# A split-precision transformer trunk: making the low part of each weight tile with ScalarE and an accumulating DMA in place of a VectorE subtraction

## The chip, the cores and the metric

The kernel runs on one core of one Trainium2 chip. The metric is the device time of one execution in microseconds (us). The program is given to five engines: PE (TensorE, matmuls), DVE (VectorE), ACT (ScalarE), POOL (GpSimd) and SP (SyncE, which here only issues DMAs).

## The reference, cut to what matters

Two layers of a causal decoder with 512 tokens of 1024 features, float32 in and out.

```python
for l in range(2):
    h = rmsnorm(x, norm_mix_g[l])
    x = x + (pool_conv_mixer(h, ...) if l % 2 == 0 else mla_attention(h, cos, sin, ...))
    x = x + memory_cross_attention(rmsnorm(x, norm_xa_g[l]), rmsnorm(mem, norm_mem_g[l]), ...)
    x = x + conv_ffn(rmsnorm(x, norm_ffn_g[l]), w_up, conv_w, conv_b, w_down)   # 1024 -> 2 * 2816 -> 1024
return rmsnorm(x, final_norm_g)
```

All linear maps are dense float32 products. The mixer holds a pooling branch and a convolution of width 31 over 512 channels; the attention of layer 1 has 16 heads; the cross-attention of both layers reads 256 memory tokens through 4 heads of 256 features.

## The kernel before

Activations lie with features on the 128 partitions and tokens along the free axis, as tiles of 128 x 512. A product runs on PE in the fast `float32r` form, which rounds its operands; to keep the precision each operand is split into a high part (the value rounded to `float32r`) and a low part (the value minus the high part). `mm3` adds three matmuls for each 128 x 128 block of weights: high by high (L157), high by low of the activations (L158), and the weights' low part by the activations' high part (L159). The low part of the weights is thus wanted as the third matmul of a tile.

Weights come in tiles of up to 128 x 1024 float32 (512 KB, eight blocks, 24 matmuls of 512 columns). `load_raw` loads one from HBM into `wr` on SP's queue (4 buffers). `load_w` makes `wh` with ACT's copy (L152) and `wl` with DVE's subtraction (L153), 3 buffers each. A buffer of `wh` comes free after the last L158 matmul of the tile three before, a buffer of `wl` after its last L159 matmul. Both lines stand under a raised priority (`AHEAD` = 40 places), so that the scheduler puts them ahead of the neighbouring work on their engines; each engine then runs its own list in order. `Linear` calls `load_w` for each tile (`lin`, and `kx` for the memory keys of layer 1); `memory_kv` calls it for the memory values (`vx`); `group` calls it for the attention's query and key weights (`uqp`, `ukv`, `uqn`). The keys of layer 0 (`kx` at L340) use the raw tile alone, and the last product (`fin`) makes its own parts at L529 and L530.

In time the kernel has these stages: the opening product and the rest of the mixer's input product, the memory keys and values of both layers beside the convolution on DVE, the mixer's output product, cross-attention, the gated MLP of layer 0 (`ffn_up`, `ffn_down`), the latent attention of layer 1, its cross-attention, the MLP of layer 1 with the final norm.

Of the kernel before, what the change touches and what calls it, by code (L numbers as in the profile page):

```python
# [15 lines left out]
ALU = mybir.AluOpType  # L16
# [47 lines left out]

# columns of the packed per-channel constants
_COLS = {}
# [15 lines left out]
def _split_2pi():  # L82
    """2*pi*512 and 2*pi cut into parts whose products with the counts below are exact in float32."""
    def head(v, bits):
        m, e = math.frexp(v)
        return math.ldexp(math.floor(m * 2 ** bits), e - bits)

    big = 2.0 * math.pi * 512.0
    parts = []
    rest = big  # L90
    for _ in range(3):
        h = head(rest, 11)
        parts.append(h)
        rest -= h
    parts.append(rest)
    d1 = head(2.0 * math.pi, 13)
    return parts, (d1, 2.0 * math.pi - d1)
# [3 lines left out]
def kernel(ctx: ExitStack, tc: tile.TileContext, a):  # L101
# [26 lines left out]

# [1 line left out]
    con = cp.tile([P, NCOL], F32, tag="con", name="con")  # L130
# [9 lines left out]

# [1 line left out]
    def load_raw(src, n):  # L142
# [4 lines left out]
    def load_w(src, n):  # L147
        raw = load_raw(src, n)
        hi = wp.tile([P, WCOLS], F32R, tag="wh", name=uid("wh"), bufs=3)
        lo = wp.tile([P, WCOLS], F32R, tag="wl", name=uid("wl"), bufs=3)  # L150
        with tc.high_priority(offset=AHEAD):
            act.copy(hi[:, :n], raw[:, :n])  # L152
            vec.tensor_tensor(lo[:, :n], raw[:, :n], f(hi[:, :n]), ALU.subtract)  # L153
        return hi, lo
# [6 lines left out]
    class Linear:  # L161
        """psum[m, t] = sum over k tiles of src[p, k * 128 + m] * xs[k][p, t], a range of k at a time."""

# [36 lines left out]
    def newton_rsqrt(v, n, name):  # L200
        """1/sqrt(v) of a narrow tile."""
        sh = small(name + "sh", [P, n], dt=I32)
        y = small(name + "y", [P, n], bufs=3)
        nv = small(name + "nv", [P, n])
        t = small(name + "t", [P, n])
        vec.tensor_scalar(sh, v.bitcast(I32), 1, None, ALU.logical_shift_right)
        vec.tensor_scalar(y.bitcast(I32), sh, -1.0, float(0x5F3759DF), ALU.mult, ALU.add)
        vec.tensor_scalar(nv, v, -0.5, None, ALU.mult)
        for _ in range(3):
            vec.tensor_tensor(t, y, y, ALU.mult)  # L210
            vec.tensor_tensor(t, t, nv, ALU.mult)
            vec.scalar_tensor_tensor(y, t, 1.5, y, ALU.add, ALU.mult)
        return y

    def col_sums(acc, n=TB):
        """sums over the partitions of acc, tokens on partitions: [128, n]."""
        ps = bank("st")
        for j in range(n):
            pe.transpose(ps[:, j * P:(j + 1) * P], acc[:, j * P:(j + 1) * P], ident)
        t = small("ssum", [P, n])  # L220
        vec.reduce_sum(t, ps[:, :n * P].rearrange("p (j c) -> p j c", c=P), axis=AX.X)
        return t

    def row_rate(src, n, name):
        """1/rms of tokens whose features lie along the free axis: [128, n]"""
        parts = small(name + "p", [P, n, 2])
        for j in range(n):
            for i in range(2):
                t = slot("nat")
                sp.dma_start(t, src[j][:, i * T:(i + 1) * T])  # L230
                act.activation(t, t, AF.Square, accum_out=parts[:, j, i:i + 1])
        v = small(name + "q", [P, n])
        vec.tensor_tensor(v, parts[:, :, 0], parts[:, :, 1], ALU.add)
        vec.tensor_scalar(v, v, 1.0 / D, EPS, ALU.mult, ALU.add)
        return newton_rsqrt(v, n, name)
# [6 lines left out]
    def spread(r, n=TB, name="rb", out=None):  # L242
        """[128, n] with tokens on partitions -> [128, n * 128] with tokens along the free axis."""
        ps = bank("rb")
# [6 lines left out]
    class Norm:  # L251
        """h = x * gain as hi and lo parts and the running sum of squares, tile by tile."""

# [37 lines left out]

# [1 line left out]
    mem_rb = cp.tile([P, MEM], F32, tag="memrb", name="memrb")  # L293
# [9 lines left out]
    class Memory:  # L303
        """the memory tokens, normalised, in two stages"""

# [25 lines left out]
    def memory_kv(layer, mg, mh, keep, native, kt, vt):  # L331
        """keys [d, mem] per head and values [mem, d]; keep takes each out of PSUM; a step per weight tile"""
        for hd in range(HX):
# [40 lines left out]

# [1 line left out]
    def cross_attention(layer, norm, kv, nxt):  # L376
# [87 lines left out]

# [1 line left out]
    def ffn(layer, norm, nxt, extra=None):  # L466
# [50 lines left out]
    def finale(layer, k0, nk):  # L517
        """the last products, half of the tokens at a time, and the final norm of each half"""
        half = T // 2
# [35 lines left out]
        def upright(k):  # L555
            """x * gain of the second half with its tokens on the partitions"""
            if not nat:
# [54 lines left out]

# [1 line left out]
    def mixer(norm, nxt):  # L614
# [6 lines left out]
        def opening(i):  # L621
            """the first product starts on the first tiles of x"""
            ps = bank("lin")
# [37 lines left out]
        def convolve():  # L661
            """the causal depthwise convolution, a tap of a tile at a time"""
            todo = [list(range(CONV_K)) for _ in range(CT - 1)] + [[s for s in range(CONV_K) if s not in PE_TAPS]]
# [17 lines left out]
        def tap_products():  # L681
            """some taps of the last tile as products with a diagonal matrix"""
            ps = bank("tap")
# [11 lines left out]
        def normalise():  # L695
            """layer norm over the channels and swish, in stages"""
            acc = slot("lacc")
# [138 lines left out]

# [1 line left out]
    def rope_tables():  # L838
# [37 lines left out]

# [1 line left out]
    SWAP = [(i + 16) % 32 for i in range(32)]  # L878
    # kinds of head: rows of the content part, rows of the rotary part, rows that stay zero
    KIND = {  # L880
# [8 lines left out]
    def latent_attention(norm, nxt, cs, sn, kv):  # L889
# [4 lines left out]

        # token factors: r * rsqrt(r^2 * mean(p^2) + eps)
        def factor(sq, dim, name):
# [13 lines left out]

        # latent projections
        kacc, acc = slot("kacc"), slot("qacc")
# [37 lines left out]
        def rotate(src, buf):  # L950
            """src holds the rotary part of four heads (PSUM or SBUF); rotated into their buffers"""
            sw = slot("sw")
# [13 lines left out]
        def contents(buf, wh, wl, xs, nk):  # L966
            """content rows of two heads per 128 output rows"""
            for i, (k0, k1) in enumerate(TILE):
# [12 lines left out]
        def group(g):  # L981
            """queries and keys of four heads"""
            rotate(linear(a["uqp"][g], cq), qb)
# [48 lines left out]
        def turn(n):  # L1032
            banks = [bank("t") for _ in range(3)]
            ts = [slot("pt") for _ in range(3)]
            # key block -> bank, first column, first query block
            place = ((0, 0, 0), (1, 0, 1), (2, 0, 2), (1, 384, 3))
# [9 lines left out]
        def values(p):  # L1046
            """a pair of heads side by side in the columns of the array"""
            ps = bank("mpv")
# [31 lines left out]

# [1 line left out]
    n0 = Norm("norm_mix_g", 0)  # L1082
# [13 lines left out]

# [1 line left out]
def _chunks(w):  # L1098
    """[K, M] -> [M/128, 128 (k within its tile), K/128 * 128]"""
    k, m = w.shape  # L1100
    return w.reshape(k // P, P, m // P, P).transpose(2, 1, 0, 3).reshape(m // P, P, k)


def _cols(v):
    """[..., n * 128] -> [128, ... * n]"""
    v = np.asarray(v)
    return v.reshape(-1, P).T
# [21 lines left out]
def _layouts(inp):  # L1129
# [21 lines left out]
    out["dq"] = _chunks(np.concatenate([dq[:, :QL + KVL]] + [dq[:, QL + KVL:]] * 4, axis=1))  # L1151
    # heads of a group of four are used in the order A, C, B, D
    uq = inp["mla_w_uq"][0].reshape(KQ, P, HEADS // 4, 4, NOPE + ROPE)
# [38 lines left out]
```

## Time and profile before

| | |
|---|---|
| three runs | 1388.11, 1388.82, 1388.9 us, median 1388.82 |
| profiled execution | span 1386.6 us from the first to the last instruction; the median of the runs is 2.2 us above this span |
| PE | 1371.6 us busy (99%) |
| DVE | 889.0 us (64%), of which 276.9 are the 240 subtractions of L153 |
| ACT | 599.2 us (43%), of which 239.0 are the 240 copies of L152 |
| POOL | 6.3 us (0%) |
| DMA | 135.28 MB, mean 98 GB/s; the load queue takes 31.0% of 16 DMA engines |

Busy times count from an instruction's start to its end. Matmuls overlap, so each lasts longer than the distance to the next; the distance is read from the number of matmuls in a stretch. Idle time is put down to the engine whose signal came last. A wait of an engine that is not the bound costs nothing by itself.

### The profile page before, as it was taken

What the parts mean: (1) busy time and instruction counts of PE and PEld (TensorE: products, weight loads), DVE (VectorE), ACT (ScalarE), POOL (GpSimd) and SP (SyncE); (2) the same over time, 40 slices, a digit from 0 to 9 for tenths busy, and PEclk for the clock granted to TensorE, in tenths of its full rate; (3) what the DMA queues carried; (4) which work ended last, traced back from release to release, by engine and by line L of the source; (5) the groups of instructions that cost most, each with busy time, mean ns of one, the idle gap of its engine ahead of it and who ended that gap; (6) DMA issues with size and microseconds to landing.
All of it is one profiled execution on the core that took longest, in us unless ns stands there. A gap on an engine that the chain in (4) does not pass through costs nothing.

```text
span 1386.6 us, 16884 instructions
## 1 busy us (share of the span) xinstructions
PE 1371.6 (99%) x6532; PEld 1131.2 (82%) x6532; DVE 889.0 (64%) x1535; ACT 599.2 (43%) x976; POOL 6.3 (0%) x17
## 2 busy tenths in 40 slices
PE   8999999999999999999999999999999999999997
PEld 6888978888888888888887776888888888888887
DVE  6999988555685366445669775755566544653565
ACT  6416456443443143223447786644443322332343
POOL 0000000000000000000100000000000000000000
PEclk9999999999999999999999999999999999999999
DMA  9235524113333333333321111321223333233221
GB/s 331 93 106 188 169 91 145 61 56 98 108 97 91 105 93 93 104 91 87 97 83 50 43 46 46 107 76 61 76 91 96 102 92 106 91 93 106 84 84 62
DMA packets 42560, 135.28 MB, mean 98 GB/s; under 512 B 4848, under 2 KB 6512, under 8 KB 42480
## 3 DMA queue, kind: packets, MB, share of 16 engines
q1 hardware_dynamic: 41904, 133.45, 31.0%
q8 instruction: 51, 0.84, 0.2%
q10 hardware_dynamic: 576, 0.76, 0.2%
q14 instruction: 29, 0.24, 0.1%
HBM read 132.09 MB, written 2.10 MB: 97 GB/s over the span
## 4 chain that ended last, share of the span: by engine, by line
PE 90%; DVE 7%; ACT 2%; issue 1%; DMA 0%; SPq 0%; DVEq 0%; ACTq 0%
PE lin L159 24%; PE lin L157 24%; PE lin L158 24%; DVE cv L677 3%; PE s L1016 1%; PE mpv L1053 1%; DVE wl L153 1%; PE t L1041 1%; PE vx L158 1%; PE vx L159 1%; PE fin L157 1%; PE vx L157 1%; PE fin L158 1%; PE fin L159 1%; ACT p L1024 1%
## 5 line engine op out<-in xcount | busy, mean ns | idle before, releaser
L152 ACT CAST wh<-wr 128x1024 fp32r<-128x1024 f32 (+3 forms) x240 | 239.0, 998 | 485.0 <-PE lin L158 338.4
L157 PE MATMUL lin<-hh,wh 128*128 128x512 f32 x976 | 382.4, 392 | 5.9 <-ACT hh L264 5.9
L158 PE MATMUL lin<-hl,wh 128*128 128x512 f32 x976 | 381.1, 391 | 0.0
L159 PE MATMUL lin<-hh,wl 128*128 128x512 f32 x976 | 380.8, 390 | 0.2 <-DVE wl L153 0.2
L153 DVE TENSOR_TENSOR wl<-wr,wh 128x1024 fp32r<-128x1024 f32 (+3 forms) x240 | 276.9, 1155 | 60.4 <-ACT wh L152 58.9
L157 PEld LDWEIGHTS lin<-hh,wh 128*128 128x128 f32 x976 | 183.8, 188 | 43.2 <-ACT hh L264 5.9
L158 PEld LDWEIGHTS lin<-hl,wh 128*128 128x128 f32 x976 | 183.7, 188 | 39.4 <-DVE hl L265 2.1
L159 PEld LDWEIGHTS lin<-hh,wl 128*128 128x128 f32 x976 | 183.7, 188 | 38.7 <-DVE wl L153 0.7
L158 PE MATMUL lin<-fl,wh 128*128 128x512 f32 x304 | 118.4, 389 | 0.0
L159 PE MATMUL lin<-fh,wl 128*128 128x512 f32 x304 | 118.3, 389 | 0.0
L157 PE MATMUL lin<-fh,wh 128*128 128x512 f32 x304 | 118.1, 389 | 0.0
L514 DVE TENSOR_TENSOR x<-x,lin 128x512 f32<-128x512 f32 x32 | 22.0, 688 | 102.8 <-PE lin L159 102.8
L479 DVE TENSOR_TENSOR g<-lin,rb 128x512 f32<-128x512 f32 x44 | 30.4, 690 | 79.2 <-PE lin L159 79.2
L677 DVE SCALAR_TENSOR_TENSOR cv<-a,con,cv 128x509 f32<-128x509 f32 (+25 forms) x115 | 79.5, 728 | 0.1
L490 DVE TENSOR_TENSOR g<-lin,rb 128x512 f32<-128x512 f32 x44 | 30.4, 691 | 71.6 <-PE lin L159 71.4
L158 PEld LDWEIGHTS lin<-fl,wh 128*128 128x128 f32 x304 | 57.1, 188 | 12.1 <-DVE fl L197 0.2
L157 PEld LDWEIGHTS lin<-fh,wh 128*128 128x128 f32 x304 | 57.1, 188 | 11.8
L159 PEld LDWEIGHTS lin<-fh,wl 128*128 128x128 f32 x304 | 57.1, 188 | 11.7
L488 ACT ACTIVATE c<-c 128x512 f32<-128x512 f32 x44 | 27.8, 633 | 82.1 <-DVE c L487 82.1
L289 DVE TENSOR_TENSOR x<-x,lin 128x512 f32<-128x512 f32 x40 | 27.3, 686 | 35.6 <-PE lin L159 35.6
L158 PE MATMUL lin<-ol,wh 128*128 128x512 f32 x128 | 50.1, 391 | 0.0
L159 PE MATMUL lin<-oh,wl 128*128 128x512 f32 x128 | 49.9, 390 | 0.0
(351 smaller groups left out, 2062.4 us busy)
## 6 DMA issues: line engine op xcount, KB each, us to landing
wr<-in_ffn_up SPq DMA_DIRECT2D x88, 512.0 KB, 3.5
wr<-in_ffn_down SPq DMA_DIRECT2D x32, 512.0 KB, 3.5
wr<-in_xa_wk SPq DMA_DIRECT2D x16, 512.0 KB, 3.7
wr<-in_xa_wv SPq DMA_DIRECT2D x16, 512.0 KB, 4.2
wr<-in_xa_wq SPq DMA_DIRECT2D x16, 512.0 KB, 3.6
wr<-in_xa_wo SPq DMA_DIRECT2D x16, 512.0 KB, 3.5
wr<-in_ffn_down SPq DMA_DIRECT2D x16, 384.0 KB, 3.1
wr<-in_pc_in SPq DMA_DIRECT2D x11, 512.0 KB, 6.6
```

Source lines behind the costliest of these rows:

```text
L152: act.copy(hi[:, :n], raw[:, :n])
L153: vec.tensor_tensor(lo[:, :n], raw[:, :n], f(hi[:, :n]), ALU.subtract)
L157: pe.matmul(ps, ah, bh, start=first, stop=False)
L158: pe.matmul(ps, ah, bl, start=False, stop=False)
L159: pe.matmul(ps, al, bh, start=False, stop=last)
L289: vec.tensor_tensor(x[m], x[m], ps, ALU.add)
L479: vec.tensor_tensor(g, gps, rb, ALU.mult)
L488: act.activation(c, c, AF.Silu)
L490: vec.tensor_tensor(g, aps, rb, ALU.mult)
L514: vec.tensor_tensor(x[m], x[m], ps, ALU.add)
L677: vec.scalar_tensor_tensor(cv[i][:, s:], gl[i][:, :T - s], w, cv[i][:, s:], ALU.mult, ALU.add)
L1016: pe.matmul(ps[i], q[:, i * P:(i + 1) * P], k[:, :P * (i + 1)], start=True, stop=True)
```

## The change

In `load_w` ACT writes minus the weights into `wl`, which rounds to minus the high part, and a DMA on POOL's queue then adds the raw weights to it, read once more from HBM. DVE no longer touches the weights (comments that were taken out are left away):

```diff
         with tc.high_priority(offset=AHEAD):
             act.copy(hi[:, :n], raw[:, :n])
-            vec.tensor_tensor(lo[:, :n], raw[:, :n], f(hi[:, :n]), ALU.subtract)
+            act.mul(lo[:, :n], raw[:, :n], -1.0)
+            pool.dma_start(lo[:, :n], src, accum_op=ALU.add)
         return hi, lo
```

The new lines shift all later line numbers by one. `act.mul` is an ACTIVATE at L153, the accumulating DMA stands at L154. There are 240 tiles: 205 of 1024 columns, 12 of 768, 19 of 512, 4 of 384, 118.0 MB in all.

In the gated MLP, ACT's list held one copy for each weight tile (`wh`), between the convolution's affine step (`c`, L485), its SiLU (L488) and the split of the product (`fh`, L196):

```order
L152 CAST wh_4403<-wr_4401 128x1024
L196 CAST fh_4321<-c_4283 128x512
L152 CAST wh_4441<-wr_4439 128x1024
L485 ACTIVATE c_4358<-g_4356,con 128x512
L488 ACTIVATE c_4358<-c_4358 128x512
L152 CAST wh_4478<-wr_4476 128x1024
```

The same place now (an earlier pass of the same loop):

```order
L152 CAST wh_4278<-wr_4276 128x1024
L153 ACTIVATE wl_4279<-wr_4276 128x1024
L197 CAST fh_4194<-c_4155 128x512
L152 CAST wh_4317<-wr_4315 128x1024
L153 ACTIVATE wl_4318<-wr_4315 128x1024
L486 ACTIVATE c_4232<-g_4230,con 128x512
L489 ACTIVATE c_4232<-c_4232 128x512
L152 CAST wh_4355<-wr_4353 128x1024
L153 ACTIVATE wl_4356<-wr_4353 128x1024
```

The negation stands right behind the copy of the same tile, and the MLP's own steps come one instruction later.

POOL's list held the identity, a constant for the mixer's norm (`om`), the causal mask and the zeros of the attention's buffers, with nothing between them:

```order
masks.py:199 AFFINE_SELECT ident<-ident 128x128
L702 MEMSET om_1609 128x128
L891 MEMSET mask_5519 128x512
L892 AFFINE_SELECT mask_5519<-mask_5519 128x128
L948 MEMSET qA_5847 32x512
```

Now the DMAs stand among them, here at the start:

```order
masks.py:199 AFFINE_SELECT ident<-ident 128x128
L154 DMA wl_94<-in_pc_in 128x512
L154 DMA wl_133<-in_pc_in 128x512
L154 DMA wl_174<-in_pc_in 128x1024
L154 DMA wl_206<-in_pc_in 128x1024
L154 DMA wl_298<-in_pc_in 128x1024
```

POOL issues 240 DMAs that were not there; each waits for ACT's negation of its tile.

SP's list of loads in the opening was, with `x` the input by features, `wr` weights of the mixer's input product, and `nat` the input by tokens, from which the first norm's rate is made:

```order
L628 DMA x_78<-in_xT 128x512
L144 DMA wr_169<-in_pc_in 128x1024
L144 DMA wr_200<-in_pc_in 128x1024
L144 DMA wr_291<-in_pc_in 128x1024
L230 DMA nat_207<-in_xN 128x512
L230 DMA nat_210<-in_xN 128x512
```

and is now:

```order
L629 DMA x_78<-in_xT 128x512
L144 DMA wr_171<-in_pc_in 128x1024
L144 DMA wr_203<-in_pc_in 128x1024
L144 DMA wr_295<-in_pc_in 128x1024
L144 DMA wr_373<-in_pc_in 128x1024
L144 DMA wr_411<-in_pc_in 128x1024
L144 DMA wr_449<-in_pc_in 128x1024
L231 DMA nat_211<-in_xN 128x512
```

Three weight loads have moved ahead of the eight `nat` loads.

ACT's list at the same place was as follows (`hh` is the high part of a tile of `x` times the gain, `dg` a diagonal for the convolution):

```order
L264 ACTIVATE hh_152<-x_77,con 128x512
L687 ACTIVATE dg_770<-ident,con 128x128
L264 ACTIVATE hh_160<-x_78,con 128x512
L152 CAST wh_171<-wr_169 128x1024
L152 CAST wh_202<-wr_200 128x1024
```

and is now:

```order
L265 ACTIVATE hh_154<-x_77,con 128x512
L152 CAST wh_173<-wr_171 128x1024
L153 ACTIVATE wl_174<-wr_171 128x1024
L152 CAST wh_205<-wr_203 128x1024
L153 ACTIVATE wl_206<-wr_203 128x1024
L265 ACTIVATE hh_162<-x_78,con 128x512
```

The last tile of `x` (`hh_162`) stands behind the fourth weight tile (`wh_205`, `wl_206`), whose buffers are those of the first tile. PE's own list is the same products in nearly the same order.

## The prediction

> **What bounds the kernel now.** I read the page's first two parts, then the stretches, then the chain and the waits. The page says first which engine has no time to give:
>
> ```profile
> span 1386.6 us, 16884 instructions
> PE 1371.6 (99%) x6532; PEld 1131.2 (82%) x6532; DVE 889.0 (64%) x1535; ACT 599.2 (43%) x976; POOL 6.3 (0%) x17
> DMA  9235524113333333333321111321223333233221
> GB/s 331 93 106 188 169 91 145 61 56 98 108 97 91 105 93 93 104 91 87 97 83 50 43 46 46 107 76 61 76 91 96 102 92 106 91 93 106 84 84 62
> ...
> q1 hardware_dynamic: 41904, 133.45, 31.0%
> ...
> PE 90%; DVE 7%; ACT 2%; issue 1%; DMA 0%; SPq 0%; DVEq 0%; ACTq 0%
> ```
>
> PE stands still for 1386.6 - 1371.6 = 15.0 us in all. The chain of work that ended last is PE for 90% and DVE for 7%. The DMA engines are busy for a third, except in the first slice and around the fourth and fifth. A busy PE need not be a full one, so I take the stretches, with the count of matmuls behind PE's busy time:
>
> ```profile
> 0.00:35.00 35.00, 28.84 (x114) 22.01 (x115) 21.66 (x38) 23.05 (x43) 0.71 (x6) 1.00 0.93 331
> 107.00:177.00 70.00, 69.94 (x398) 61.27 (x397) 69.60 (x92) 37.79 (x53) 0.00 (x0) 1.00 0.55 178
> 310.00:680.00 370.00, 370.00 (x1637) 306.29 (x1637) 210.22 (x278) 128.68 (x158) 2.08 (x4) 1.00 0.32 96
> 735.00:840.00 105.00, 104.28 (x561) 76.55 (x560) 84.64 (x263) 83.77 (x193) 0.00 (x0) 1.00 0.18 55
> ```
>
> The columns after the length are PE, PEld, DVE, ACT, POOL, the clock, the DMA share and GB/s. In the gated MLP (310 to 680) a matmul comes every 370 / 1637 = 0.226 us without a gap. A weight tile of 24 matmuls lasts 24 x 0.226 = 5.42 us there, and DVE has 43% to spare. So taking work off DVE buys nothing in the MLPs; what matters is whether `wl` still arrives in time. In the opening the DMA engines are the full resource: 331 GB/s at a share of 0.93, or 331 / 0.93 = 356 GB/s if they never rest. By this a full tile of 0.524 MB takes 0.524 / 356 = 1.47 us of all 16 engines.
>
> **The change, part by part.** What moves, and what prices it:
>
> ```profile
> L152 ACT CAST wh<-wr 128x1024 fp32r<-128x1024 f32 (+3 forms) x240 | 239.0, 998 | 485.0 <-PE lin L158 338.4
> L153 DVE TENSOR_TENSOR wl<-wr,wh 128x1024 fp32r<-128x1024 f32 (+3 forms) x240 | 276.9, 1155 | 60.4 <-ACT wh L152 58.9
> ...
> wr<-in_ffn_up SPq DMA_DIRECT2D x88, 512.0 KB, 3.5
> ...
> nat<-in_xN SPq DMA_DIRECT2D x8, 256.0 KB, 7.2
> ...
> wr<-in_pc_in SPq DMA_DIRECT2D x2, 256.0 KB, 4.1
> ```
>
> 1. DVE loses 240 instructions, 276.9 us. ACT gains 240 of the same shapes as its copies, 239.0 us, to 838 of 1387 (60%). ACT waits 338.4 us for PE in front of the copies, and PE's bound hides the rest outside the attention.
>
> 2. POOL gains 240 DMAs of 118.0 MB. No POOL-issued and no adding DMA is in this trace. I call r the engine time of one against a plain load of the same bytes. It is not below 1, since it carries the same bytes in. At the far end reading the weights, reading what stands in `wl`, adding and writing cost a whole plain transfer each, r = 4. I take r = 2, because such a DMA has two inbound streams where the rows show one. Landing is then the plain 3.5 us, plus 1.47 for the second stream, plus up to 1.47 when a raw load shares the engines: 6.4 us. For POOL's issue I take 1.0 us, between SP's 0.33 and the 1.9 at which SP's full queue issues (9.35 us for 5 in the opening):
>
> ```profile
> 15.56 9.35 SPq L144 DMA_DIRECT2D wr<-in_pc_in  x5
> 507.25 1.05 ACT L152 CAST wh<-wr 128x1024 fp32r<-128x1024 f32 x1 [3.06 <-PE lin L158]
> 508.21 0.81 ACT L485 ACTIVATE c<-g,con 128x512 f32<-128x512 f32 x1
> 772.51 65.27 SPq L144 DMA_DIRECT2D wr<-in_mla_o  x7
> ```
>
> The Trainium skill, "DMA: Bandwidth & Descriptors" (Anatomy of one DMA), fits a POOL-issued DMA as 2.0 us plus bytes at 436 GB/s, an estimate of 3.2 us for 512 KB, which would be the hidden case below. "Collectives: The Full Stack" (The bandwidth ceiling) says a reducing DMA runs at half the rate because it needs two source reads, with a measured ratio of 1.93. It would give my sum, and nothing in this trace decides between the two pages.
>
> 3. *The MLPs and the other products with tiles of 24 matmuls.* PE releases a buffer and ACT, idle 3.06 us before, copies at once. Then 1.05 copy, 1.05 negation, 1.0 issue, 6.4 landing: 9.5 us. The low part is wanted two tiles and two matmuls later, 2 x 5.42 + 0.45 = 11.3 us. Engine time is (1 + 2) x 1.47 = 4.4 us in 5.42. So nothing is lost, with 1.8 us to spare. What stands behind the negation on ACT (`c`) goes 1.05 us later; its product is used only when its group of tiles is complete.
>
> 4. *The memory keys and values, 107 to 177.*
>
> ```profile
> 107.00:177.00 70.00, 29.20 (x25) 1.00 0.55 178
> L340 PE MATMUL kx<-mg,wr x128: 377/379/379, 75.7 to 107.2; 128*128 128x256 f32 x128
> ```
>
> The first row counts the subtractions: 25 tiles in 70 us, 2.8 us each, because a value tile feeds only 12 wide matmuls. Raw loads need 178 x 70 / 356 = 35 us of engine time, the 25 tiles 25 x 1.47 x 2 = 73.6 more: 109 in 70. Ahead of it the keys of layer 0 use raw tiles only (second row), so three tiles can be ready, 3 x 3 x 1.47 = 13 us. Lost: 109 - 70 - 13 = 26 us. Here PE waits for `wl`, and DVE, full now with 69.6 of 70, no longer matters.
>
> 5. *The mixer's output product* has 16 half tiles of 12 matmuls, 2.7 us each; the way from release to landing (0.6 + 0.6 + 1.0 + 2.0 + 3 x 0.74) is 6.4 against 2 x 2.7 + 0.45 = 5.9, a third of 0.5 for each, some 2 us.
>
> 6. *The opening.*
>
> ```profile
> 3.85 0.62 ACT L152 CAST wh<-wr 128x512 fp32r<-128x512 f32 x1 [0.90 <-DMA wr<-in_pc_in]
> 4.50 0.69 DVE L153 TENSOR_TENSOR wl<-wr,wh 128x512 fp32r<-128x512 f32 x1 [4.50 <-ACT wh L152]
> 7.32 0.63 PE L159 MATMUL lin<-hh,wl 128*128 128x512 f32 x1
> 8.29 6.87 SPq L230 DMA_DIRECT2D nat<-in_xN  x8
> 21.02 0.16 DVE L233 TENSOR_TENSOR rxq<-rxp 128x4 f32<-128x4 f32 x1 [3.38 <-ACT nat L231]
> 26.18 0.44 PE rb L246 x4
> ```
>
> The first L159 matmul starts at 7.32. Now: copy ends 4.5, negation 5.1, issue 6.1, landing 4.1 plus 0.74 later, 10.9: PE is 3.6 us late. Nine more matmuls end the first tile near 14; the fourth tile's negation waits for that and ends near 15, and the last tile of `x` stands behind it. SP's eighth weight load needs the buffer which that negation frees, and the eight `nat` loads, issued from 8.29 before, stand behind that load: 6.7 us later. The rate was ready shortly before PE used it (`rb`, 26.18). It moves by these 6.7, by some 3 for the two full accumulations that share the engines and by 2 to 3 negations among ACT's squares, less about 1.3 of slack: 11 us in all. The loads in their sum say the same: 7 full tiles x 2 x 1.47 = 20.6 us more in a stretch with 35 x 0.07 = 2.5 to spare and 9.8 of loads ahead of need.
>
> 7. *The attention, 735 to 840.* ACT gets what DVE loses here, 13 tiles and some 12 us (first row below), and goes from 83.8 to about 96 of 105 us. ACT's exponentials feed DVE and PE in turn there, so I charge half, 6.
>
> ```profile
> 735.00:840.00 105.00, 12.72 (x13) 1.00 0.18 55
> 736.58 0.95 DVE L153 TENSOR_TENSOR wl<-wr,wh 128x768 fp32r<-128x768 f32 x1
> L157 PE MATMUL nope<-cqh,wh x24: 389/389/389, 737.6 to 825.1; 128*128 128x512 f32 x24
> 747.07 1.14 DVE wl L153
> 768.84 1.13 DVE wl L153
> 771.62 0.87 DVE wl L153
> ```
>
> The first group's query tile is used 0.1 us after its subtraction (second and third row), and would land some 4 us later. Three subtractions of 3.1 us stand in the chain and go. 6 + 4 - 3 = 7 us.
>
> 8. POOL's own list: its memsets wait for DVE, and DMAs stand behind them.
>
> ```profile
> 666.08 0.52 POOL L948 MEMSET qA<- 32x512 f32 x1 [461.57 <-DVE g L490]
> 693.34 0.52 POOL L948 MEMSET kD<- 32x512 f32 x1 [4.03 <-DVE acc L275]
> ```
>
> The zeros were all written by 693.9, over 30 us before the attention's tiles are used. Cost nothing; if they came 30 us later the key tiles would hang on them.
>
> Sum: 11 + 26 + 2 + 7 = +46 us on the span of 1386.6, that is 1433. The median of the runs, 1388.82, is 2.2 above the span: 1435.
>
> **The rivals.** *The addition is dearer and the DMA engines become the bound.* It decides from r = 5.42 / 1.47 - 1 = 2.7, where a full tile no longer fits beside PE's time. At r = 3 each of some 175 full tiles outside opening and memory stage loses 0.47 (82 us), the memory stage 62, the opening 14, the rest 13: 1560. At r = 4 they are 341, 99, 17 and 25: 1871. For it: no row prices the addition. Against: one third of the engines' time is all that plain loads take.
>
> *The transfer is hidden anyway*, r near 1. The memory stage then needs 35 + 37 = 72 us, less its lead: nothing. The opening keeps 8, since the late `nat` loads hardly depend on r, the attention 5: 1402, at best 1390.
>
> *Faster.* DVE's freed time shortens the attention, the one place where its subtractions stand between PE's pieces: 3 us there, and 2 in other gaps of the 15.0 that PE has: 1384. It decides only if the opening loses under 5 us; the order of the loads speaks against that.
>
> *POOL issues late.* If an issue took 3.5 us in place of 1.0, because POOL has to wait for DVE's instructions of 0.7 to 1.2 us, the way would be 12.0, over 11.3: 0.7 / 3 for each of 175 tiles, 41 us: 1476. Against it: POOL idles now and DVE is at 64%, at 44% after. The Trainium skill, "SBUF — State Buffer" (SBUF: two separate sides), describes such a lockout of POOL's descriptor writing while DVE runs certain copies; no run here shows it yet.
>
> **How the numbers follow.** The forecast (r from 1.5 to 2.6) 49%, the dearer addition 25%, hidden 14%, faster 6%, late issue 6%. The predicted time is the likeliest case's, 1435; its own range is 1412 (r = 1.5: 10 + 7 + 0 + 6) to 1461 (r = 2.6: 13 + 48 + 3 + 8). The range of 80% goes from 1392, below which lie the faster case and a little of the hidden one, to 1750, above which lies the part of the dearer case with r over 3.6, about 10%. A measurement can tell about 0.2% from no change. Faster 0.06; same 0.05, from the hidden case; slower 0.89.
>
> **What would show it.** Right: L153 gone from DVE, an ACT group of about 240 us at `wl`, a POOL queue of about 118 MB; PE idle before L159 in the memory stage, waiting for a DMA to `wl`; `rb` near 37 us; MLP stretches still at 0.226 us a matmul. DMA share there near 0.32 x 3 = 0.96 by the rows' unhurried share, or 0.8 by 4.4 of 5.42. Wrong: PE waiting for `wl` in every MLP tile (r over 2.7, or landing over 8 us), or no wait at all in the memory stage.

## The result and the profile after

The changed kernel takes 1499.75 us, the median of four runs (1498.9 to 1502.47), against 1388.64 for the kernel before on the same chip: 1.0805 times as long (95% interval 1.079 to 1.082), 111 us slower. The forecast was 46 us slower. The direction held; the size was more than twice what I had summed. The time lies inside the wide range of 1392 to 1750 only by luck: it is above the likeliest case's own range (1412 to 1461), and the wide range reached that far for the sake of the dearer addition, which is not what happened.

The page of the changed kernel, its busy times, the granted clock, the two large DMA queues and the chain of work that ended last:

```profile
span 1497.1 us, 17423 instructions
PE 1402.3 (94%) x6532; PEld 1146.6 (77%) x6532; DVE 639.3 (43%) x1295; ACT 807.9 (54%) x1216; POOL 213.2 (14%) x257
PEclk9999799999999999999999999999999999999999
...
q0 software_dynamic: 34560, 117.98, 44.0%
q1 hardware_dynamic: 41904, 133.45, 31.0%
...
PE 50%; issue 29%; DMA 10%; POOL 4%; DVE 3%; ACT 2%; SPq 0%; POOLq 0%; DVEq 0%; ACTq 0%
```

PE now stands still for 1497.1 - 1402.3 = 94.8 us, against 15.0. It also counts 30.7 us more busy for the same 6532 matmuls, so some of them ran slower. The adding DMAs are a queue of their own (q0): 117.98 MB, or 225 full tiles, for 44.0% of the span. That is 658.7 us of all 16 engines and 2.93 us for a full tile.

The groups of the new work, and the medians from issue to landing:

```profile
L153 ACT ACTIVATE wl<-wr 128x1024 fp32r<-128x1024 f32 (+3 forms) x240 | 240.1, 1000 | 23.6 <-PE vx L159 23.6
...
L154 POOL DMA_DIRECT2D wl<-in_ffn_up x88 | 76.1, 865 | 408.2 <-ACT wl L153 401.7
```

```profile
wl<-in_ffn_up POOLq DMA_DIRECT2D x88, 512.0 KB, 7.6
...
wl<-in_xa_wv POOLq DMA_DIRECT2D x16, 512.0 KB, 7.6
...
wl<-in_xa_wk POOLq DMA_DIRECT2D x8, 512.0 KB, 8.7
...
wl<-in_pc_out POOLq DMA_DIRECT2D x16, 256.0 KB, 4.9
...
nat<-in_xN SPq DMA_DIRECT2D x8, 256.0 KB, 11.6
```

What PE waited for, in total, times, and the longest:

```profile
PE vx L159 <- DMA wl<-in_xa_wv: 22.4, 13, 7.1
PE kx L160 <- DMA wl<-in_xa_wk: 12.7, 4, 4.7
PE lin L160 <- DMA wl<-in_pc_in: 7.8, 2, 4.8
PE lin L158 <- ACT hh L265: 6.2, 1, 6.2
PE rb L247 <- DVE rmy L213: 5.3, 1, 5.3
PE lin L160 <- DMA wl<-in_mla_o: 4.7, 2, 4.4
PE nope L160 <- DMA wl<-in_uqn: 4.6, 1, 4.6
PE lin L160 <- DMA wl<-in_xa_wo: 4.3, 2, 2.2
PE lin L160 <- DMA wl<-in_pc_out: 3.8, 5, 1.3
PE rb L247 <- DVE rxy L213: 3.6, 1, 3.6
PE lin L160 <- DMA wl<-in_xa_wq: 3.5, 1, 3.5
PE lin L160 <- DMA wl<-in_ffn_up: 3.0, 1, 3.0
```

Only the wait for `hh` was there before (5.9 us). The rest are waits for a low part, or for one of the two rates of the opening (`rxy`, the first norm; `rmy`, the memory tokens). The 88 tiles of `ffn_up` cost one wait of 3.0 us in all.

To see where the time went I took the start of the same PE work in both traces. The difference of neighbouring rows is what the stage between them lost:

| event on PE | before | after | later by | lost since the row above |
|---|---|---|---|---|
| `rb` of the first norm | 26.0 | 39.5 | 13.5 | 13.5 |
| first native key product (`kx`, L341) | 75.7 | 97.1 | 21.4 | 7.9 |
| last `vx` product | 177.0 | 247.7 | 70.7 | 49.3 |
| first token sums for cross-attention (`st`) | 228.6 | 310.0 | 81.4 | 10.7 |
| first `rb` of the first MLP | 349.1 | 432.5 | 83.4 | 2.0 |
| first `nope` product of the attention | 734.9 | 824.6 | 89.7 | 6.3 |
| last `nope` product | 825.5 | 924.0 | 98.5 | 8.8 |
| last scores of the second cross-attention (`sx`) | 966.5 | 1074.1 | 107.6 | 9.1 |
| `rb` of the second MLP | 1026.0 | 1136.0 | 110.0 | 2.4 |
| last `fin` product | 1376.8 | 1486.8 | 110.0 | 0 |

Two of the rows from which the table is made, with first and last start (the native keys and the last value products):

```profile
L341 PE MATMUL kx<-mg,wr x128: 377/379/379, 97.1 to 128.6; 128*128 128x256 f32 x128
```

```profile
L160 PE MATMUL vx<-wh,ml x64: 387/393/632, 132.6 to 247.7; 128*128 128x512 f32 x64
```

Some stretches by engine, in the order of the prediction's (length, PE, PEld, DVE, ACT, POOL, clock, DMA share, GB/s), opening, memory stage, attention and second MLP:

```profile
0.00:39.50 39.50, 21.91 (x72) 16.23 (x72) 8.09 (x22) 24.84 (x43) 6.03 (x12) 0.96 0.90 274
...
128.60:247.70 119.10, 83.93 (x397) 68.48 (x396) 33.42 (x52) 59.11 (x76) 21.78 (x26) 0.89 0.90 212
...
824.60:924.00 99.40, 92.72 (x470) 68.13 (x468) 67.06 (x223) 78.06 (x176) 8.90 (x11) 0.97 0.40 89
...
1136.00:1450.00 314.00, 314.00 (x1388) 260.11 (x1387) 104.66 (x149) 155.67 (x183) 48.30 (x56) 1.00 0.89 190
```

The second MLP is as full as before: 1388 matmuls in 314 us, 0.226 us each. The memory stage is the other extreme: the 70 us have become 119.1, of which PE is idle for 35.2, and its clock is 0.89.

The chain in the memory stage shows both (start, length, what):

```profile
157.61 7.99 DMA wl<-in_xa_wv
165.60 0.04 issue
165.64 0.80 PE vx L159
166.44 0.43 PE vx L160
166.86 0.43 PE vx L159
...
169.85 0.43 PE vx L160
...
171.05 0.23 PE vx L159
...
172.89 0.24 PE vx L159
173.13 0.01 POOLq L154
173.14 7.35 DMA wl<-in_xa_wk
180.49 0.04 issue
180.54 0.39 PE kx L160
```

An addition lands at 165.6 and PE starts after 7.07 us of idleness. For 4.6 us its matmuls come 0.43 us apart in place of 0.23. The addition that goes out at 173.14 is that of the next key tile, and the chain puts its wait down to the L159 product that ends just before it. ACT's list shows what it more likely waited for, its own negation, which ends at 172.85:

```profile
170.31 1.05 ACT L152 CAST wh<-wr 128x1024 fp32r<-128x1024 f32 x1 [5.57 <-PE vx L160]
...
171.79 1.06 ACT L153 ACTIVATE wl<-wr 128x1024 fp32r<-128x1024 f32 x1
```

The three additions before it also went out 0.29 to 0.30 us after the end of their negations. PE's last product with the value tile at 165.6 releases ACT at 170.3; copy, a cast, negation, issue and landing follow, 10.2 us until 180.5. In between PE works on the tiles that are there, and then stands idle for 4.2 us.

### The profile page after: what moved, and what is told of

It reads as the page before. It is cut to its first block, busy times and chain, and to the rows that moved or that the text cites. A ratio compares the mean times of both kernels' runs of the same rounds, so it can differ in the third digit from the quotient of the medians.

```text
span 1497.1 us, 17423 instructions
## 1 busy us (share of the span) xinstructions
PE 1402.3 (94%) x6532; PEld 1146.6 (77%) x6532; DVE 639.3 (43%) x1295; ACT 807.9 (54%) x1216; POOL 213.2 (14%) x257
## 3 DMA queue, kind: packets, MB, share of 16 engines
q0 software_dynamic: 34560, 117.98, 44.0%
## 4 chain that ended last, share of the span: by engine, by line
PE 50%; issue 29%; DMA 10%; POOL 4%; DVE 3%; ACT 2%; SPq 0%; POOLq 0%; DVEq 0%; ACTq 0%
PE lin L160 13%; PE lin L158 13%; PE lin L159 13%; POOL wl L154 4%; DMA wl<-in_xa_wv 3%; DVE cv L678 2%; DMA wl<-in_xa_wk 1%; PE s L1017 1%; DMA wl<-in_xa_wo 1%; DMA nat<-in_memN 1%; PE fin L158 1%; PE fin L159 1%; PE fin L160 1%; DMA nat<-in_xN 1%; PE mpv L1054 1%
## 5 line engine op out<-in xcount | busy, mean ns | idle before, releaser
L159 PE MATMUL lin<-hl,wh 128*128 128x512 f32 x976 | 383.5, 393 | 0.0
L153 ACT ACTIVATE wl<-wr 128x1024 fp32r<-128x1024 f32 (+3 forms) x240 | 240.1, 1000 | 23.6 <-PE vx L159 23.6
L159 PEld LDWEIGHTS lin<-hl,wh 128*128 128x128 f32 x976 | 185.5, 190 | 39.0 <-DVE hl L266 0.8
L154 POOL DMA_DIRECT2D wl<-in_ffn_up x88 | 76.1, 865 | 408.2 <-ACT wl L153 401.7
L159 PE MATMUL lin<-fl,wh 128*128 128x512 f32 x304 | 118.3, 389 | 0.0
L515 DVE TENSOR_TENSOR x<-x,lin 128x512 f32<-128x512 f32 x32 | 22.0, 688 | 142.8 <-PE lin L160 142.8
L480 DVE TENSOR_TENSOR g<-lin,rb 128x512 f32<-128x512 f32 x44 | 30.4, 691 | 105.8 <-PE lin L160 98.2
L159 PEld LDWEIGHTS lin<-fl,wh 128*128 128x128 f32 x304 | 57.1, 188 | 11.9
L487 DVE SCALAR_TENSOR_TENSOR c<-g,con,c 128x511 f32<-128x511 f32 x44 | 33.1, 751 | 72.3 <-ACT c L486 72.3
L266 DVE SCALAR_TENSOR_TENSOR hl<-x,con,hh 128x512 fp32r<-128x512 f32 x48 | 36.0, 751 | 59.6 <-ACT hh L265 59.4
L154 POOL DMA_DIRECT2D wl<-in_ffn_down x40 | 34.5, 863 | 176.3 <-ACT wl L153 169.7
```

The source lines that it names most:

```text
L153: act.mul(lo[:, :n], raw[:, :n], -1.0)
L154: pool.dma_start(lo[:, :n], src, accum_op=ALU.add)
L159: pe.matmul(ps, ah, bl, start=False, stop=False)
L266: vec.scalar_tensor_tensor(l, x[k], g, f(h), ALU.mult, ALU.subtract)
L480: vec.tensor_tensor(g, gps, rb, ALU.mult)
L487: vec.scalar_tensor_tensor(c[:, 1:], g[:, :T - 1], w(1), c[:, 1:], ALU.mult, ALU.add)
```

## The experiments

The code below is shortened, and some names are changed. I had three theories. A: PE waits for a low part that lands late. B: the traffic itself makes all loads late. C: ACT's second pass is what costs. Within A, two things could set the pace: the engines' sum of time, or the way from a buffer's release to the landing, against a ring of three.

**A spare tile that nobody reads.** DVE subtracts for PE as before; ACT and the DMA do the new work beside it.

```diff
+            vec.tensor_tensor(lo[:, :n], raw[:, :n], f(hi[:, :n]), ALU.subtract)
-            act.mul(lo[:, :n], raw[:, :n], -1.0)
-            pool.dma_start(lo[:, :n], src, accum_op=ALU.add)
+            act.mul(spare[:, :n], raw[:, :n], -1.0)          # 3 buffers, SLOTS = 53
+            pool.dma_start(spare[:, :n], src, accum_op=ALU.add)
```

> DVE makes the low parts that PE uses, as before; ACT's negation and the adding DMA work as in the changed kernel, but on a spare tile (3 buffers; the working slots are 53 in place of 58 to make room) that nobody reads. So the traffic, ACT's load and POOL's queue stay and only PE's wait for the DMA goes. Theory A (PE's wait for the late low part costs nearly all): 1395 to 1420 us, with some 10 to 20 us left in the opening, where the loads stand in another order. Theory B (the traffic itself costs, because raw loads come late): over 1470. Theory C (ACT's second pass costs): over 1440.

Measured: 1493.06 us, 1.0757 (1.0737 to 1.0776). Theory A's range is missed, and those of B and C are met: though PE reads nothing that an addition writes, the kernel is almost as slow. ACT's group and its largest waits in this run:

```profile
L155 ACT ACTIVATE wd<-wr 128x1024 fp32r<-128x1024 f32 (+3 forms) x240 | 240.7, 1005 | 269.2 <-DMA wr<-in_ffn_up 76.9
```

The negation of the spare tile (`wd`) stands in front of later copies on ACT and sat idle for 269.2 us; in the changed kernel the same group had 23.6. The profile puts most of it down to the raw load, which the copy ahead of the negation had already read; that it was the buffer, held until its addition had landed, is argued and not shown. So this run had made a wait of its own. It does not say whether traffic or ACT is to blame, nor does it refute A. The next runs take the two apart. First, the five activation buffers that it gave away:

> The kernel before with 53 in place of 58 activation buffers, nothing else. It is the control for the spare-tile runs, which gave five buffers away. If the buffers do not matter: 1386 to 1395 us, and the spare-tile run's extra time belongs to its negations and additions. If the missing buffers made that run slow: over 1420 us.

Measured: 1388.34 us, 0.9999 (0.9989 to 1.0008). The buffers do not matter.

**ACT's second pass alone.** ACT negates, DVE adds the raw tile, no adding DMA.

```diff
             act.mul(lo[:, :n], raw[:, :n], -1.0)
-            pool.dma_start(lo[:, :n], src, accum_op=ALU.add)
+            vec.tensor_tensor(lo[:, :n], raw[:, :n], f(lo[:, :n]), ALU.add)
```

> ACT's negation stays, DVE adds the raw tile to it, no DMA on POOL. Theory A: 1390 to 1400 us, the attention's 5 to 7 us and nothing else. Theory B: the same. Theory C (ACT's second pass and its order): over 1430.

Measured: 1405.28 us, 1.0121 (1.0104 to 1.0138). ACT's pass costs 17 us, 8.8 of them before the native keys (84.5 us in place of 75.7), 3.3 in the memory stage, 0 in the MLPs and in the attention (90.4 us in place of 90.6). It is a little above what A and B had expected, and it is not the 111. The 8.8 are not ACT's alone: in this run the `nat` loads go out at 16.39 us in place of 8.29, behind two more weight loads, so that the order of SP's loads is part of it.

**The traffic alone.** DVE subtracts, ACT has its copies alone, and POOL adds each weight tile to one of three fixed spare tiles, after a copy of one column of `wh` that ties it to ACT's copy.

```diff
+            vec.tensor_tensor(lo[:, :n], raw[:, :n], f(hi[:, :n]), ALU.subtract)
-            act.mul(lo[:, :n], raw[:, :n], -1.0)
-            pool.dma_start(lo[:, :n], src, accum_op=ALU.add)
+            pool.tensor_copy(spare[:, :1], f(hi[:, :1]))     # SLOTS = 52
+            pool.dma_start(spare[:, :n], src, accum_op=ALU.add)
```

> DVE subtracts and PE uses its result, as in the kernel before; ACT has its copies alone. POOL adds each weight tile once more from HBM into one of three spare tiles that nobody reads, issued when ACT's copy of that tile is done (a one-column copy on POOL waits for it). So the crowd on the DMA engines is there, without ACT's second pass and without a low part that PE waits for. Theory B (the crowded engines make the raw loads late): the opening loses 8 to 20 us and the memory stage 20 to 45, the MLPs nothing: 1420 to 1455. Theory D (in the first spare-tile run it was ACT's ordered list, where a negation that waits for a buffer holds up the copies behind it): the traffic alone costs under 15 us, 1389 to 1404. If it is as slow as the first spare-tile run, over 1480, the traffic is the whole cause.

Measured: 1422.03 us, 1.0241 (1.0226 to 1.0256), theory B's range. The native keys start at 90.5 us, 14.8 late. The memory stage takes 81.8 us:

```profile
31.20:61.80 30.60, 26.16 (x105) 21.25 (x106) 21.05 (x42) 11.51 (x18) 7.62 (x11) 0.89 0.99 246
...
122.00:203.80 81.80, 73.62 (x398) 60.99 (x398) 68.42 (x88) 36.79 (x50) 35.98 (x42) 1.00 1.05 276
```

The share of the DMA engines is 0.99 and 1.05 there (the time of packets is summed, so it can pass 1). They are full, and the plain loads come late (a value tile lands after 10.8 us in place of 4.2). The opening lost what I had expected, the memory stage 11.8 us and not 20 to 45, and some 6 more went in the stretch behind it. From 262 us on the run loses nothing more. So the same bytes cost 33 us where nobody waits for them, all of it early.

**The stages, one by one.** `wl` by DVE for the memory keys and values alone; and, in another run, for all that comes before the mixer's output product (input, pooling, memory).

```diff
+            if <tile of the stages named>:
+                vec.tensor_tensor(lo[:, :n], raw[:, :n], f(hi[:, :n]), ALU.subtract)
+            else:
                 act.mul(lo[:, :n], raw[:, :n], -1.0)
                 pool.dma_start(lo[:, :n], src, accum_op=ALU.add)
```

> The changed kernel, with the 24 tiles of the memory keys and values (kx, vx) made by DVE as before. In the changed kernel this stage took 119.1 us in place of 70. Theory A: those 49 us come back, nearly alone: 1448 to 1455. If the stage only passed on a delay which another stage would then show: over 1470.

Measured: 1451.17 us, 1.0452 (1.0437 to 1.0468): the 49 us come back.

> The changed kernel, with DVE's subtraction kept for the mixer's input weights, the pooling weights and the memory keys and values (56 of 240 tiles); all tiles from the mixer's output product on by negation and adding DMA. If the losses of each stage are its own: the opening and the memory stage give back 21 + 49 us, what is left is the 40 us found behind 206 us in the changed kernel: 1424 to 1434. If what was lost late in the program was carried over from the early stages: 1389 to 1410.

Measured: 1433.7 us, 1.0326 (1.0307 to 1.0346). The native keys start at 76.7 us and the last `vx` product at 178.0, 1.0 late each. What is left is the late loss, 45 us, where the changed kernel has 39 behind the last `vx` product. The losses of the stages are their own and add up to within some 6 us.

**Four and five buffers of each part.**

```diff
-        hi = wp.tile([P, WCOLS], F32R, tag="wh", name=uid("wh"), bufs=3)
-        lo = wp.tile([P, WCOLS], F32R, tag="wl", name=uid("wl"), bufs=3)
+        hi = wp.tile([P, WCOLS], F32R, tag="wh", name=uid("wh"), bufs=4)   # then 5
+        lo = wp.tile([P, WCOLS], F32R, tag="wl", name=uid("wl"), bufs=4)   # SLOTS = 55, 51
```

> The changed kernel with 4 buffers in place of 3 for the high and the low part (working slots 55 in place of 58). If the way from release to landing (latency) is what PE waits for, one more tile of lead takes away most of the waits outside the opening: 1440 to 1460. If the 16 DMA engines are the limit where PE waits (the memory stage needs 109 us of them by the prediction's sum, and took 119), at most 10 us come back there and some 15 in the other stages: 1470 to 1490.

> The changed kernel with five buffers of each part (and 51 activation buffers). With three the memory stage took 119 us, with four 101. If the way from release to landing against the ring is what paces it: 84 to 92 us, and the whole 1422 to 1433. If the engines' sum paces it (109 us less what is loaded ahead and what overhangs): 94 to 101 us, and the whole 1436 to 1446.

Measured: 1445.18 us with four, 1.0412 (1.0392 to 1.0431), and 1433.96 with five, 1.0321 (1.0307 to 1.0335). The memory stage with four, then with five:

```profile
126.90:228.30 101.40, 79.82 (x397) 65.42 (x396) 35.00 (x55) 61.72 (x81) 22.64 (x27) 0.93 1.02 255
```

```profile
130.40:224.80 94.40, 77.80 (x398) 61.66 (x397) 34.01 (x53) 62.15 (x81) 23.56 (x28) 0.98 1.06 272
```

And the landing of the value tiles in the same two runs:

```profile
wl<-in_xa_wv POOLq DMA_DIRECT2D x16, 512.0 KB, 9.7
```

```profile
wl<-in_xa_wv POOLq DMA_DIRECT2D x16, 512.0 KB, 11.7
```

With three buffers the engines are at 0.90 and an addition lands in 7.6 us; with four at 1.02 and in 9.7; with five at 1.06 and in 11.7. So at three the ring paces the stage: the next addition can't be issued. From four on the engines are full, and each further buffer mostly makes a longer queue in front of them. Five gave 94.4 us, the low end of what I had expected if the engines' sum sets it; the whole came out just above the other theory's range.

**Additions only where they might be free.** The late stages with four buffers, DVE elsewhere:

> DVE's subtraction up to the memory stage, negation and adding DMA from the mixer's output product on, with four buffers of each part (and 55 activation buffers). The run with additions only after the memory stage lost 45 us, the four-buffer run lost 6 of its 58 behind 206 us. If latency against the ring of three is what costs behind the memory stage: 1391 to 1398 us. If the traffic or ACT's second pass costs there: over 1405.

Measured: 1392.86 us, 1.0035 (1.0022 to 1.0048). A fourth buffer takes the 45 us of late losses down to 4, with the traffic and ACT's second pass as they were. So neither of the two costs there by itself; what costs is a low part that is late against the ring of three.

**Two value tiles ahead of the native keys.**

```diff
     def memory_kv(layer, mg, mh, keep, native, kt, vt):
+        lead = [load_w(a["xa_wv"][layer, 0, kk], 2 * T) for kk in range(2 if native else 0)]
...
-                wh, wl = load_w(a["xa_wv"][layer, half, kk], 2 * T)
+                wh, wl = lead.pop(0) if lead else load_w(a["xa_wv"][layer, half, kk], 2 * T)
```

> The changed kernel with the first two value tiles of layer 0 loaded, negated and added ahead of the native keys, so that the memory stage (128.6 to 247.7 us in the changed kernel) starts with two tiles ready, as the prediction had assumed of three. If the missing lead is part of the mis-sized term: two tiles at 4.4 to 4.7 us and most of the first wait of 3.5 us, so the stage lasts 106 to 111 us in place of 119.1 and the whole is 8 to 13 us faster than the changed kernel: 1486 to 1492. If the stage is paced by something that a lead does not shorten (the pooling weights hold one of the three buffers up to 155 us in the changed kernel): under 4 us, 1496 or more.

Measured: 1493.36 us, 1.0752 (1.0736 to 1.0768). The stage runs from 123.35 to 235.9, 112.5 us: 6.6 less, between the two expectations. The missing lead is real and smaller than I had put it.

**Keeping PE's clock up.** Six matmuls that nobody reads, ahead of each key and value tile of the memory stage:

```diff
+                for i in range(6):
+                    pe.matmul(dummy, wh[:, :P], wh[:, :T], start=i == 0, stop=i == 5)
```

> The changed kernel, with six matmuls (0.23 us each, 144 in all, 33 us) whose result nobody reads ahead of each of the 24 key and value tiles of the memory stage, so that PE works through most of the 35 us that it stood idle there. If the slow spacing of matmuls after each stall (0.43 us for 0.23, clock 0.89 in the stage) costs the 14 us that I counted: the stage takes 105 to 113 us in place of 119.1. If the adding DMAs pace the stage, the slow matmuls lie beside the next tile's transfer and cost nothing: 117 to 124 us.

Measured: 1498.76 us, 1.0805 (1.0787 to 1.0823), no change of the whole that can be told from noise.

```profile
128.00:242.90 114.90, 107.03 (x541) 88.99 (x540) 33.35 (x52) 59.64 (x77) 21.84 (x26) 0.99 0.95 222
```

With 144 more matmuls the clock is 0.99 in place of 0.89 and the stage 4.2 us shorter, between the two expectations. PE was busy for 83.93 - 69.94 = 14.0 us more in this stage than in the kernel before, and these are the 14 that I had counted. Removing the slow matmuls gives back some 4 of them, net of what the extra matmuls cost themselves, so 4 is a lower bound. The rest probably lay beside the next tile's transfer.

**The order of SP's loads.** The eight loads of the input by tokens are written one product earlier (`row_rate` called behind the first product in place of the second); two weight loads then stand behind them.

> The changed kernel with the eight loads of the input by tokens written one product earlier, so that two of the weight loads that stood ahead of them on SP's queue stand behind. If the order of SP's queue makes the opening late: the first norm's rate is spread (rb) at 28 to 34 us in place of 39.5, and the whole is 4 to 12 us faster than the changed kernel, 1487 to 1496. If the opening's loss is the sum of its bytes: rb moves, but the first key product still starts near 97 us and the whole stays within 3 us of 1499.

Measured: 1495.82 us, 1.0764 (1.0746 to 1.0782). The `nat` loads go out at 9.97 us in place of 19.32. `rb` comes at 36.4, 3.1 us earlier and not at the 28 to 34 expected, and the native keys at 91.9, 5.2 us earlier. The order is a part of the opening's loss, a quarter.

**The addition read from SBUF.**

```diff
-            pool.dma_start(lo[:, :n], src, accum_op=ALU.add)
+            pool.dma_start(lo[:, :n], raw[:, :n], accum_op=ALU.add)
```

> The changed kernel, whose adding DMA reads the raw tile from its buffer in place of HBM; the raw buffer is held until the addition has landed. If the price (2.93 us of all 16 engines for a full tile) comes from three streams through the engines wherever they come from: 2.7 to 3.1 us, landing 7 to 8 us. If the read from HBM is the dear part: under 2.5 us and landing under 6.5. The raw buffers, held some 8 us longer, make the loads wait in both cases: 1500 to 1540 us by the first, 1460 to 1500 by the second.

> The changed kernel with four buffers and the addition read from the raw tile's buffer. The engines' time for a tile is the same in both forms (2.95 against 2.93 us), only the landing is shorter (5.8 against 7.5 us). If the way paces the early stages: the memory stage 85 to 95 us and the whole 1410 to 1430. If the engines' sum does: 97 to 102 us and 1436 to 1446.

Measured: 1461.04 us, 1.0531 (1.0506 to 1.0556). The queue and the landing:

```profile
q0 software_dynamic: 34560, 117.98, 45.5%
...
wl<-wr POOLq DMA_DIRECT2D x205, 512.0 KB, 5.8
```

45.5% of 1458.3 us over 225 tiles is 2.95 us, the same engine time as from HBM, as the first expectation had it; the landing and the whole are the second's. The landing is shorter by some 1.7 us, and plain loads land earlier too (4.7 us in place of 5.7 for `ffn_up`). Together this gives back 39 us: 8 in the opening, 10 in the memory stage, 21 later. With four buffers it gives back nothing: 1446.85 us, 1.0412 (1.0398 to 1.0426), against 1445.18 read from HBM. The memory stage took 105.4 us, above both ranges; the whole is just above the range for the engines' sum. With four buffers a shorter way no longer helps.

**A version that might beat the kernel before.** From its first to its last `nope` product the attention took 89.5 us in the run with four buffers and 89.6 in the one with late additions alone, against 90.6 before, so it could be the one place that gains.

> The kernel before with four buffers of each part, with the negation and the adding DMA only for the 12 weight tiles of the attention's heads. In the runs with four buffers that stage took 1.1 to 1.3 us less than in the kernel before, since three subtractions leave the chain there. If that gain stands by itself: 1386.6 to 1388.0, a ratio of 0.998 to 0.9995. If it came from later loads around it: 1388 to 1390.

Measured: 1388.38 us, 0.9996 (0.9987 to 1.0005). The stage takes 89.4 us against 90.6, but it starts 1.1 us later, and the end is where it was. No version that was tried beats the kernel before by more than the noise.

## Why the prediction was right or wrong

**Right: the price of the addition in engine time.** I took r = 2, 2.94 us for a full tile; it is 2.93. The dearer addition and the hidden transfer, which lived on another r, are out. Against a plain load that is 2.93 / 1.47 = 1.99. The Trainium skill, "Collectives: The Full Stack" (The bandwidth ceiling), has a measured 1.93 between a gather, which copies, and a reduce-scatter, which needs two source reads; the 1.99 of this trace agrees with it. POOL's issue was put at 1.0 us and is 0.86, so the late issue is out too.

**Right: the MLPs.** The second MLP lost 0, the first, with its beginning and the projections behind it, 6.3, of which one wait in the MLP is 3.0 (below). The way with the measured landing is 1.05 + 1.05 + 0.87 + 7.6 = 10.6 us, still under 11.3.

**Near by luck: the attention, step 7, 7 us in the sum, 8.8 measured.** Its first query tile waited 4.6 as said (4) and the key tiles 1.7; slower matmuls make up 2.8. The 6 us charged for ACT's second pass show in no run: with that pass alone the stage took 90.4 us, with four buffers 89.5, against 90.6 before. The 3 us for the subtractions that leave the chain were at most 1.1. Two terms were wrong and nearly cancelled with what the step had left out.

**Mis-sized: the landing**, 6.4 us in the sum, 7.6 measured. The Trainium skill, "DMA: Bandwidth & Descriptors" (Anatomy of one DMA), whose fit gave an estimate of 3.2, is further off for an adding DMA beside other traffic.

**Mis-sized: the memory stage, step 4, 26 us in the sum, 49.3 measured.** The step added up engine time and left out the check that steps 3 and 5 make, the way against the ring of three. A ring of three gives one tile for each third of negation, issue, landing and use. By my own terms that is (1.05 + 1.0 + 6.4 + 2.8) / 3 = 3.75 us, 94 us for 25 tiles, no more than the 70 + 26 = 96 of the sum. So the check alone would not have saved the forecast; the terms in it failed. By the measured ones, with a landing between the 7.6 and 8.7 of value and key tiles, it is (1.05 + 0.87 + 8.15 + 2.8) / 3 = 4.3, or 107, and the engines' sum without its lead is 109. The limits are that near, and the runs show that at three buffers the ring paces: the engines are at 0.90, and the stage takes 119.1 us with three buffers, 101.4 with four, 94.4 with five. That my 96 is near the last is no proof of the sum, which holds 13 us of lead that the changed kernel did not have. The 12 us from 107 to 119.1 are not settled. In the stretch shown, the copy and a cast stand between release and negation (170.31 to 171.79), 1.5 us that neither formula has; a third of it for 25 tiles would be those 12, an estimate from one tile. Two smaller parts of the loss have runs of their own. The lead of 13 us did not exist, since the raw buffers were full of native key tiles (the first value tile's addition was issued at 124.6 us, four before the stage began); two tiles ahead give back 6.6. And PE's clock falls in the long waits, worth at least 4.2. These parts overlap and don't add up exactly. POOL's list shows the missing lead; it waited 36.1 us for ACT's first negation of the stage:

```profile
124.57 0.86 POOL L154 DMA_DIRECT2D wl<-in_xa_wv  x1 [36.10 <-ACT wl L153]
```

**Mis-sized: the opening, step 6, 11 us in the sum, 21.4 measured.** The step followed the first norm's rate, and at its `rb` the kernel is 13.5 us late, not far from 11. (The check by the loads' sum, 20.6 - 2.5 - 9.8, gives 8.3 and not 11.) The other 7.9 come behind it, where I had put nothing: the rate of the memory tokens comes from the same queue and was late as well, a wait of 5.3 us. Within the 13.5 the parts are less sure. The `nat` loads went out 11.0 us later, not 6.7, yet with most of that undone `rb` came only 3.1 us earlier. The traffic alone, with the `nat` loads in their old place, made `rb` 5.2 us late, for the 3 charged. With ACT's pass alone it was 5.9 late, but there the `nat` loads had moved too; what ACT costs by itself in the opening stays open.

**Left out: mostly the first tiles of a stage, 2 + 0 in the sum, some 30 measured.** I priced the ring's steady state (step 3), where two tiles are always ahead. At a change of stage, as I read POOL's list, PE arrives with less than two ahead or with half tiles behind it: the first query tile of cross-attention (3.5), `xa_wo` (4.3 in two waits), `mla_o` (4.7 in two). One wait of 3.0 us lies in the middle of the first MLP, and it shows how another late load gets to PE. DVE stood waiting for the load of the token positions (`pos`, for the rotary tables of layer 1), which landed after 8.1 us in place of 4.3. DVE's list had the rotary steps ahead of the MLP's `g`, ACT's next step waited for that `g`, and the next copy and negation stood behind that step in ACT's list:

```profile
465.27 0.43 DVE L845 CAST ang<-pos 128x512 f32<-128x512 int32 x1 [7.33 <-DMA pos<-in_pos]
...
470.05 0.82 ACT L486 ACTIVATE c<-g,con 128x512 f32<-128x512 f32 x1 [7.90 <-DVE g L480]
...
480.10 0.50 PE L160 MATMUL lin<-hh,wl 128*128 128x512 f32 x1 [3.00 <-DMA wl<-in_ffn_up]
```

With the mixer's output product, priced at 2 and waiting for 3.8, these are the stretches of the 10.7, 2.0, 6.3, 9.1 and 2.4 of the table: some 21 us in which PE is idle, and 9 of slower matmuls. A fourth buffer removes nearly all of it.

What stays open: why the spare-tile run lost 105 us where its two parts alone lost 17 and 33. The long waits of its negations fit a back-up in ACT's ordered list, but no run took that wait away by itself. Open too are the shares within the opening and the last 12 us of the memory stage.

## What to carry to other kernels

Price a transfer that replaces a computation twice in every stage: by the sum of engine time, and by the way from a buffer's release to the landing against the depth of the ring, with the tile that is used up fastest and with the first tile after each change of stage. The larger of the two counts, and here one more buffer was worth 55 us. Work that an idle engine does in its own ring (DVE at 64%) is not worth moving to a path with 10 us of latency when neither engine is the bound.

## What the runs showed of the hardware

In these kernels an adding DMA of 512 KB costs 2.93 us of all 16 engines from HBM and 2.95 from SBUF, but lands after 7.6 or 5.8 us (medians): the source changed the latency, not the load.

After 7.07 us of idleness PE's matmuls of 512 columns came 0.43 us apart for 4.6 us, then 0.23. The Trainium skill, "TensorE: Matmul & The Clock Gate" (What's actually happening), describes this halving after an idle window of some 3.4 us, and the trace agrees. What I had not expected is how little came back when the waits were filled with other matmuls, about 4 us of a stage of 119.
